# Gathering expert tokens for two pairs at once, in split precision, and reading gates and transposed one-hots from a selector product

## The chip, the cores and the metric

The kernel runs on one NeuronCore of a Trainium2 chip, as one program with one launch. The metric is the time of one execution on the device, in microseconds (us); lower is better. The reference times are the median of three executions.

## The reference, cut to what matters

One encoder layer, in float32: a mixing sub-layer (short convolution and latent attention), a cross-attention into a memory, and a mixture of 16 experts in which each expert picks its 64 tokens out of 512. The change touches only the last one.

```
h    = rmsnorm(x2, norm_moe_g)                        # x2: 512 tokens x 1024
aff  = softmax(h @ w_router)                          # 512 x 16
gates, idx = top_k(aff.T, 64)                         # per expert: 64 tokens and their gates
xg   = h[idx]                                         # 16 x 64 x 1024
a    = silu(xg @ w_gate) * (xg @ w_up)                # per expert, 1024 x 1024 each
yo   = (a @ w_down) * gates
x3   = x2 + zeros.at[idx].add(yo)                     # scatter
out  = rmsnorm(x3, norm_final_g)
```

## The kernel before, in words

The 512 tokens lie in four tiles of 128 partitions (NT = 4), the 1024 columns in eight blocks of 128 (KT = 8). Every engine runs its instructions in the order in which the code is written; nothing is rescheduled. Weights arrive by DMA in chunks of 1 MiB (128 x 2048 float32). Such a chunk lies in one of 22 slots (`NSLOT`); slots are handed out first in, first out. Every load is issued from SP's queue, in order, and an issue waits until the last reader of its slot is done. `load_experts(reserve)` (line 171 issues) hands out slots as long as more than `reserve` are free.

The experts come in eight pairs. A pair needs 24 chunks: 16 of gate and up weights, 8 of down weights. The stages of a pair are:

- `gather(p)` (lines 1241 to 1250): DVE makes a one-hot matrix `oh` (tokens x 128 picked places), multiplies it by the token's rstd into `ohr`, and TensorE multiplies x2 by it in plain float32, 4 products for each of the 8 column blocks. DVE scales each block by the norm's gain out of PSUM into `xg`.
- `gu_half` (lines 1281 and 1282): the gate and up products of half an expert, two products side by side on 64 columns of the array each; then ACT's silu (`sg`, line 1293) and DVE's product (`act`, line 1294).
- `pair_prep` (lines 1259 to 1268): the gates `gcol` and the transposed one-hot `oht` from four float32 products and four transposes of `oh`.
- `combine` (lines 1384 and 1386): the scatter of the pair before, as products with `oht`, added by DVE into `acc`.
- `down` (line 1362): four groups of 16 TensorE instructions, one for each half of the columns and of the depth. `some(each, GB)` runs two column blocks of the next pair's gather behind each group. Ahead of the first group the code runs two blocks (`some(gat, GA)`).

A plain float32 product is issued as two TensorE instructions here; a product of float32r operands as one. Elsewhere in the kernel a float32 operand is split into a float32r part and its rest (`split`, lines 119 and 120), and the products of the parts are summed. The first two experts go through `gu_wide`, with the gather of pair 0 woven between their products. Scratch tiles of 128 x 512 come from a ring of eight (`scr`), `xg` tiles from a ring of three (`mini`).

Of the kernel before, what the change touches and what calls it, by code (L numbers as in the profile page):

```python
# [18 lines left out]
KT = 8  # L19
NT = 4  # L20
# [6 lines left out]
NSLOT = 22  # L27
SPLIT_AHEAD = 2

MEM_RESERVE, RES_MM, RES_X = 4, 0, 2  # L30
MO0, MOP = 25, 4
LAG, PJ = 3, 5
GA, GB = 2, 2
WARM3, WARM, WARM2, TOP0, EV1, EV2, EV3 = 1, 4, 2, 1, 1, 2, 1


# [2 lines left out]
S_ID = S_WR + KT * E  # L39
S_SEL = S_ID + 128  # L40
S_IOTA = S_SEL + E
S_N = S_TRI = S_IOTA + C


ENTRIES = ([("cq", 0), ("cq", 1), ("ckv", 0), ("kr", 0)]
# [18 lines left out]
def layer_kernel(ctx: ExitStack, tc: tile.TileContext, x, mem, small, rope, dense, experts, out):  # L64
# [167 lines left out]
    def some(g, n):  # L232
        for _ in range(n):
            next(g, None)
# [4 lines left out]
    def col(o):  # L239
        return sm[:, o:o + 1]  # L240
# [964 lines left out]
    V.tensor_reduce(last[:, 2, 0:1], last[:, 1], axis=AX.X, op=OP.min)  # L1205


    b = Bank("warm")
    keep_warm(b, WARM)
    bt = Bank("thr")  # L1210
# [17 lines left out]
    V.tensor_tensor(pos, flag, cum, op=OP.mult)  # L1228
    V.tensor_tensor(plT, pos[:, 0], pos[:, 1], op=OP.add)
    bc.free()  # L1230
    keep_warm(b, WARM2)
    b.free()
    iota = sm[:, S_IOTA:S_IOTA + C]

    XG, gcol, OH, OHT = {}, {}, {}, {}

    def gather(p):

        w0 = OH[p] = scr(name="oh").rearrange("p (a c) -> p a c", a=NT)
        w = scr(name="ohr").rearrange("p (a c) -> p a c", a=NT)  # L1240
        V.tensor_tensor(w0.rearrange("p a (e c) -> p a e c", e=2),
                        plT[:, :, 2 * p:2 * p + 2, None].to_broadcast([128, NT, 2, C]),
                        iota[:, None, None, :].to_broadcast([128, NT, 2, C]), op=OP.is_equal)
        V.tensor_tensor(w, w0, r2[:, :, None].to_broadcast([128, NT, 128]), op=OP.mult)  # L1244
        XG[p] = mini(FT, "xg").rearrange("p (k c) -> p k c", k=KT)
        for k in range(KT):
            b = Bank("xg")
            for a in range(NT):
                PE.matmul(b.t[:, 0:128], xt[a][:, k * 128:(k + 1) * 128], w[:, a], start=a == 0, stop=a == NT - 1)  # L1249
            V.tensor_scalar(XG[p][:, k], b.t[:, 0:128], col(S_GMOE + k), None, op0=OP.mult)  # L1250
            b.free()
            yield

    def pair_prep(p):

        w = OH.pop(p)
        b = Bank("gcol")
        for a in range(NT):
            PE.matmul(b.t[:, 0:2], w[:, a], aff[:, a, 2 * p:2 * p + 2], start=a == 0, stop=a == NT - 1)
        gcol[p] = tiny(name="gcol")  # L1260
        V.tensor_copy(gcol[p][0:64], b.t[0:64, 0:1])
        V.tensor_copy(gcol[p][64:128], b.t[64:128, 1:2])
        b.free()
        b = Bank("oht")
        for a in range(NT):
            PE.transpose(b.t[:, a * 128:(a + 1) * 128], w[:, a], ident)
        OHT[p] = scr(FR, "oht")
        A.copy(OHT[p], b.t)
        b.free()


# [30 lines left out]
        gu_part(e, b, 1)  # L1302
        gu_evac(e, b, n)

    def gu_wide(e, then):

        bs = [Bank("gu") for _ in range(2)]
        for k in range(KT):
            c = xraw.popleft()
            spare = (e, k) == (0, SPARE)  # L1310
            w = c if spare else [c.t[:, j * 512:(j + 1) * 512] for j in range(4)]
            lt = XG[0][:, k, e * C:(e + 1) * C]
            for n in range(2):
                PE.matmul(bs[n].t[0:64], lt, w[n], start=k == 0, stop=k == KT - 1)  # L1314
                PE.matmul(bs[n].t[64:128], lt, w[2 + n], start=k == 0, stop=k == KT - 1)
            if not spare:
                c.free()
            load_experts(RES_X)
            then(k)
        for n in range(2):  # L1320
            gu_evac(e, bs[n], n)

    def act_trans(p, n):

        s = act.pop((p, n))
        b = Bank("actT")
        for j in range(4):
            PE.transpose(b.t[:, j * 128:(j + 1) * 128], s[:, j * 128:(j + 1) * 128], ident)
        aT[p, n] = scr(name="aT").rearrange("p (j c) -> p j c", j=4)
        w = b.t.rearrange("p (j c) -> p j c", j=4)  # L1330
        if n == 0:
            A.copy(aT[p, n], w)  # L1332
        else:
            for h in range(2):
                V.tensor_copy(aT[p, n][:, 2 * h:2 * h + 2], w[:, 2 * h:2 * h + 2])
        b.free()
# [34 lines left out]
                b.free()  # L1371
        return ys, yv

    acc_s, acc = [], []

    def combine(p, ys, yv):
        if p == 0:
            acc_s.extend(Slot(FT, "acc") for _ in range(2))
            acc.extend(acc_s[a // 2].v("a d", a=2)[:, a % 2] for a in range(NT))
        for a in range(NT):  # L1380
            for n in range(2):
                b = Bank("cb")
                for s in range(2):
                    PE.matmul(b.t, OHT[p][:, a * 128:(a + 1) * 128], yv[:, n, s], start=s == 0, stop=s == 1)  # L1384
                c = slice(n * 512, (n + 1) * 512)
                V.tensor_tensor(acc[a][:, c], b.t, (acc if p else xt)[a][:, c], op=OP.add)
                b.free()
        ys.free()

# [41 lines left out]
        if n == 1 and k == 2:  # L1431
            tail_half0(yv, [3])

    gat = gather(0)
    for _ in range(2):
        next(gat)
    pend = None
    for p in range(NP):
        last = p == NP - 1
        for q in range(2):  # L1440
            e = 2 * p + q
            if e == 0:
                gu_wide(0, lambda k: next(gat, None))
                continue
            if e == 1:
                gu_wide(1, lambda k: pair_prep(0) if k == 5 else None)
            else:
                gu_half(e, 0)
            if q == 0:
                pair_prep(p)  # L1450
                if pend is not None:
                    combine(*pend)
                    pend = None
                if last:
                    for s in xs:
                        s.free()
                    gf = Slot(FT, "gf").t
            if last and q == 1:
                preload(0)
                preload(1)  # L1460
            if e > 1:
                gu_half(e, 1, mid=(lambda: act_trans(p, 0)) if q else None)
            if last and q == 0:
                spread_gain(0)
                spread_gain(1)
        gat = iter(()) if last else gather(p + 1)
        some(gat, GA)
        if p == 0:
            act_trans(0, 0)

        def mid():
            act_trans(p, 1)
            if last:
                load_table(AF.Sqrt)

        pend = (p, *down(p, mid, gat, then=tail if last else None))
# [101 lines left out]
def _small(i):  # L1578
    s = np.zeros((128, S_N + 128), np.float32)

    def put(o, v):
        v = v.reshape(-1, 128).T
        s[:, o:o + v.shape[1]] = v

    put(S_GMIX, i["norm_mix_g"][0])
    put(S_CW, i["conv_w"][0])
    put(S_CB, i["conv_b"][0])
    put(S_QG, i["q_norm_g"][0])
    put(S_KVG, i["kv_norm_g"][0])
# [10 lines left out]
    s[:, S_IOTA:S_TRI] = np.arange(1, C + 1)  # L1600
    return s


# [27 lines left out]
```

## Time and profile before

| What | us |
|---|---|
| median of 3 executions (lowest to highest) | 1184.69 (1184.65 to 1189.49) |
| the profiled execution | 1183.84 |
| its span, first to last instruction | 1182.1 |

The profiled execution is 1.74 us longer than its span (start and end outside the program's own instructions) and 0.85 us below the median. The expert stage begins near 680 us and its last gate and up product ends near 1145 us. The views give times from the span's start. PE is TensorE, PEld its weight loads, DVE VectorE, ACT ScalarE, POOL GpSimd, SP the queue that issues the loads.

### The profile page before, as it was taken

The numbers are of one execution on the slowest core, as the hardware profiler recorded it, in microseconds if no ns is written. First come the engines' busy times: TensorE is split into PE (matmuls) and PEld (weight loads), VectorE is DVE, ScalarE is ACT, GpSimd is POOL, SyncE is SP. The second block draws the span as 40 slices with busy tenths as digits, with TensorE's granted clock in tenths as the row PEclk, the third lists the DMA queues.
The fourth block names the chain that finished last, engine by engine and source line by source line (L and its number), as shares of the span: only waits on it lengthen the run. The fifth ranks groups of instructions, "written<-read, shape, count | busy, mean of one in ns | idle before, by whom it ended". The sixth has DMA issues, their size and how long they took to land.

```text
span 1182.1 us, 13968 instructions
## 1 busy us (share of the span) xinstructions
PE 1135.1 (96%) x5715; PEld 767.9 (65%) x5715; DVE 500.0 (42%) x958; ACT 356.6 (30%) x648; POOL 1.2 (0%) x5
## 2 busy tenths in 40 slices
PE   8999999999999999999999798999999999999995
PEld 5888888888788888898888544444443444343432
DVE  6567452322687665564555712213121212121204
ACT  6223231223898734563434200101000000000013
POOL 0000000000000000000000000000000000000000
PEclk9999999999999999999999899999999999999998
DMA  8233222322010444244246788999999999999931
GB/s 345 72 107 107 72 83 96 107 107 72 1 36 2 143 143 178 72 143 142 72 179 230 311 306 325 361 399 403 421 408 421 420 422 417 421 402 421 421 144 72
DMA packets 38927, 265.95 MB, mean 225 GB/s; under 512 B 4432, under 2 KB 4816, under 8 KB 8016
## 3 DMA queue, kind: packets, MB, share of 16 engines
q1 hardware_dynamic: 38720, 265.00, 57.1%
q8 instruction: 45, 0.74, 0.3%
q14 instruction: 18, 0.15, 0.0%
q10 hardware_dynamic: 144, 0.07, 0.0%
HBM read 262.95 MB, written 2.10 MB: 224 GB/s over the span
## 4 chain that ended last, share of the span: by engine, by line
PE 92%; DVE 4%; ACT 3%; DMA 0%; issue 0%; SPq 0%; DVEq 0%
PE gu L1281 16%; PE y L1362 10%; PE xg L1249 6%; PE mm L205 4%; PE mq L205 4%; PE mo L205 4%; PE mix L205 4%; PE co L205 4%; PE gb L205 4%; PE gc L205 4%; PE gcv L205 4%; PE xc L205 4%; PE gml L205 4%; PE gu L1314 2%; PE cb L1384 2%; PE mk L205 2%
## 5 line engine op out<-in xcount | busy, mean ns | idle before, releaser
L1282 PE MATMUL gu<-xw,xg 128*64 128x512 f32 x448 | 196.8, 594 | 0.0
L1281 PE MATMUL gu<-xw,xg 128*64 128x512 f32 x448 | 196.8, 594 | 0.0
L120 DVE TENSOR_TENSOR ent<-raw,ent 128x1024 fp32r<-128x1024 f32 (+2 forms) x113 | 129.1, 1155 | 92.0 <-ACT ent L119 91.8
L1281 PEld LDWEIGHTS gu<-xw,xg 128*64 128x64 f32 x448 | 60.1, 137 | 123.4 <-issue 120.8
L1362 PE MATMUL y<-xw,aT 128*64 128x512 f32 x512 | 121.3, 608 | 0.7 <-ACT aT L1332 0.7
L119 ACT CAST ent<-raw 128x1024 fp32r<-128x1024 f32 (+2 forms) x113 | 109.0, 995 | 0.1
L1294 DVE TENSOR_TENSOR act<-gu,sg 64x512 f32<-64x512 f32 x32 | 22.2, 694 | 186.5 <-ACT sg L1293 186.4
L1249 PEld LDWEIGHTS xg<-ohr,x 128*128 128x128 f32 x512 | 63.5, 201 | 49.4 <-DVE ohr L1244 26.2
L1249 PE MATMUL xg<-ohr,x 128*128 128x128 f32 x512 | 70.6, 293 | 20.5 <-DVE ohr L1244 20.5
L1293 ACT ACTIVATE sg<-gu 64x512 f32<-64x512 f32 x32 | 18.8, 588 | 213.3 <-PE gu L1282 179.3
L1250 DVE TENSOR_SCALAR xg<-xg,small 128x128 f32<-128x128 f32 x64 | 22.5, 351 | 136.9 <-PE xg L1249 136.9
L1362 PEld LDWEIGHTS y<-xw,aT 128*64 128x64 f32 x512 | 34.9, 140 | 65.0 <-issue 61.4
L1369 ACT ACTIVATE y<-y,gcol 128x512 fp32r<-128x512 f32 x16 | 11.0, 687 | 183.7 <-PE y L1362 183.7
L1282 PEld LDWEIGHTS gu<-xw,xg 128*64 128x64 f32 x448 | 60.0, 137 | 0.0
L205 PE MATMUL mm<-ent,mo 128*128 128x512 f32 x192 | 48.4, 399 | 0.0
L205 PE MATMUL gc<-hT,ent 128*128 128x512 f32 x192 | 44.8, 389 | 0.0
L205 PE MATMUL gb<-hT,ent 128*128 128x512 f32 x192 | 44.8, 389 | 0.0
L205 PE MATMUL xc<-hT,ent 128*128 128x512 f32 x192 | 44.8, 389 | 0.0
L205 PE MATMUL gcv<-hT,ent 128*128 128x512 f32 x192 | 44.8, 389 | 0.0
L205 PE MATMUL co<-yT,ent 128*128 128x512 f32 x192 | 44.8, 389 | 0.0
L205 PE MATMUL mq<-hm,ent 128*128 128x512 f32 x192 | 44.7, 390 | 0.0
L205 PE MATMUL mo<-o,ent 128*128 128x512 f32 x192 | 44.7, 391 | 0.0
(277 smaller groups left out, 1695.7 us busy)
## 6 DMA issues: line engine op xcount, KB each, us to landing
xw<-in_experts_dram SPq DMA_DIRECT2D x189, 1024.0 KB, 9.4
raw<-in_dense_dram SPq DMA_DIRECT2D x52, 1024.0 KB, 4.8
x<-in_x_dram SPq DMA_DIRECT2D x8, 512.0 KB, 4.5
xw<-in_experts_dram SPq DMA_DIRECT2D x4, 512.0 KB, 12.1
out_dram<-out SPq DMA_DIRECT2D x4, 512.0 KB, 2.6
raw<-in_dense_dram SPq DMA_DIRECT2D x2, 512.0 KB, 8.2
mem<-in_mem_dram SPq DMA_DIRECT2D x1, 1024.0 KB, 4.8
xs<-in_experts_dram SPq DMA_DIRECT2D x4, 256.0 KB, 15.0
```

Source lines behind the costliest of these rows:

```text
L119: A.copy(hi, src)
L120: V.tensor_tensor(lo, src, f32(hi), op=OP.subtract)
L205: PE.matmul(self.o, lhsT, rhs, start=self.k == 0, stop=self.k == self.n - 1)
L1249: PE.matmul(b.t[:, 0:128], xt[a][:, k * 128:(k + 1) * 128], w[:, a], start=a == 0, stop=a == NT - 1)
L1250: V.tensor_scalar(XG[p][:, k], b.t[:, 0:128], col(S_GMOE + k), None, op0=OP.mult)
L1281: PE.matmul(b.t[0:64], lt, wg[:, k], start=kk == 0, stop=kk == KT - 1)
L1282: PE.matmul(b.t[64:128], lt, wu[:, k], start=kk == 0, stop=kk == KT - 1)
L1293: A.activation(sg[64:128], b.t[0:64], AF.Silu)
L1294: V.tensor_tensor(act[p, n][q * 64:q * 64 + 64], b.t[64:128], sg[64:128], op=OP.mult)
L1314: PE.matmul(bs[n].t[0:64], lt, w[n], start=k == 0, stop=k == KT - 1)
L1362: PE.matmul(b.t[q * 64:q * 64 + 64], aT[p, kh][:, kk, q * C:(q + 1) * C], w[:, kk], start=k == 0, stop=k == KT - 1)
L1384: PE.matmul(b.t, OHT[p][:, a * 128:(a + 1) * 128], yv[:, n, s], start=s == 0, stop=s == 1)
```

## The change

- Two gather products share one pass. `gather(ps)` takes a list of pairs: 1 and 2 behind pair 0, 3 and 4 behind pair 2, 5 and 6 behind pair 4, 7 alone behind pair 6. The one-hots of two pairs lie side by side in one float32r tile `oh` (from `mini`), so that the moving operand has 256 columns. Pair 0 keeps the old form (`gather_first`).
- The stationary operand is x2 times rstd, computed once into two slots `xn` (`norm_x2`, eight ACT instructions during expert 1), and split into a float32r part and its rest for each column block, two blocks ahead (`part`, tiles `xp`, one ACT cast and one DVE subtraction each).
- The product of a block is then eight instructions of 128 x 256. DVE scales the first pair's half into `xg`, ACT the second's.
- Ahead of the first `down` group there is no gather product any more, only the preparation.
- Gates and `oht` come from row tables: `tr` holds the affinities (float32r part and rest) and the tokens' places as 16 rows each, made once by transposes. For each pair POOL writes a selector `sel`, two products of 128 x 512 spread the pair's rows, DVE compares one with the place number (`oht`) and multiplies and sums the other (`gcol`).
- The scatter adds into x2 itself; the two `acc` slots are gone. The slots kept back by `load_experts` go from 2 to 1 (none during expert 0).

```diff
-MEM_RESERVE, RES_MM, RES_X = 4, 0, 2
+MEM_RESERVE, RES_MM, RES_X = 4, 0, 1
...
+    b_aff = to_rows(aff)
+    A.copy(tr[0:E], b_aff.t[0:E])
...
+    b_pl = to_rows(plT)
+    A.copy(tr[64:64 + E], b_pl.t[0:E])
+    b_pl.free()
     keep_warm(b, WARM2)
...
+    def to_rows(src):
+        b = Bank("rows")
+        for a in range(NT):
+            PE.transpose(b.t[0:E, a * 128:(a + 1) * 128], src[:, a], ident)
+        return b
...
+    def gather(ps):
+
+        w = len(ps) * 128
+        oh = mini(FR, "oh").rearrange("p (a c) -> p a c", a=NT)
+        for i, p in enumerate(ps):
+            one_hot(oh[:, :, i * 128:i * 128 + 128], p)
+            new_xg(p)
+        parts = {}
+
+        def part(k):
+            if k < KT:
+                parts[k] = [scr(FR, "xp").rearrange("p (a c) -> p a c", a=NT) for _ in range(2)]
+                split(xn[k // 4][:, :, k % 4 * 128:k % 4 * 128 + 128], *parts[k])
+
+        part(0)
+        part(1)
+        yield
+        for k in range(KT):
+            b = Bank("xg")
+            m = Mac(b.t[:, 0:w], 2 * NT)
+            for x in parts.pop(k):
+                for a in range(NT):
+                    m.one(x[:, a], oh[:, a, 0:w])
+            for i, p in enumerate(ps):
+                src = b.t[:, i * 128:i * 128 + 128]
+                if i == 0:
+                    V.tensor_scalar(XG[p][:, k], src, col(S_GMOE + k), None, op0=OP.mult)
+                else:
+                    A.activation(XG[p][:, k], src, AF.Copy, scale=col(S_GMOE + k))
+            b.free()
+            part(k + 2)
+            yield
...
-        w = OH.pop(p)
-        b = Bank("gcol")
-        for a in range(NT):
-            PE.matmul(b.t[:, 0:2], w[:, a], aff[:, a, 2 * p:2 * p + 2], start=a == 0, stop=a == NT - 1)
...
+        b = rows(64, 64 + E)
+        OHT[p] = scr(FR, "oht")
+        V.tensor_scalar(OHT[p], b.t, col(S_PIO), None, op0=OP.is_equal)
+        b.free()
+        b = rows(0, 32 + E)
         gcol[p] = tiny(name="gcol")
+        V.scalar_tensor_tensor(b.t, b.t, 1.0, f32(OHT[p]), op0=OP.mult, op1=OP.mult, accum_out=gcol[p])
...
-        gat = iter(()) if last else gather(p + 1)
-        some(gat, GA)
+        gat = gather(range(p + 1, min(p + 3, NP))) if p % 2 == 0 and not last else iter(())
         if p == 0:
             act_trans(0, 0)
+        next(gat, None)
```

What moves on the engines is shown at three places. The first is TensorE at the end of pair 4 (experts 8 and 9), before the change: `gu` is the last gate and up product, `xg` the gather for pair 5, `y` the first `down` group.

```order
L1282 MATMUL gu_6707<-xw_6581,xg_6462 64x512
L1249 MATMUL xg_6747<-ohr_6743,x_3169 128x128 x2
L1249 MATMUL xg_6747<-ohr_6743,x_3170 128x128 x2
L1249 MATMUL xg_6753<-ohr_6743,x_3169 128x128 x2
L1249 MATMUL xg_6753<-ohr_6743,x_3170 128x128 x2
L1362 MATMUL y_1110_6760<-xw_6583,aT_6725 64x512
```

And TensorE at the same place in the changed program (between the second row and the last four stand the other seven `y` products of the first group).

```order
L1348 MATMUL gu_6745<-xw_6611,xg_6207 64x512
L1428 MATMUL y_1131_6794<-xw_6624,aT_6763 64x512
...
L206 MATMUL xg_6805<-oh_6780,xp_6785 128x256 x4
L206 MATMUL xg_6805<-oh_6780,xp_6786 128x256 x4
L206 MATMUL xg_6820<-oh_6780,xp_6789 128x256 x4
L206 MATMUL xg_6820<-oh_6780,xp_6790 128x256 x4
```

The products that need DVE's one-hot no longer stand between the last `gu` and the first `y`; a whole `down` group stands ahead of them.

The second place is DVE beside it, before the change.

```order
L1294 TENSOR_TENSOR act_6675<-gu_6707,sg_6739 64x512
L1241 TENSOR_TENSOR oh_6742<-plT_5419,small_75 128x512
L1244 TENSOR_TENSOR ohr_6743<-oh_6742,r_721_4967 128x512
L1250 TENSOR_SCALAR xg_6746<-xg_6747,small_75 128x128
L1250 TENSOR_SCALAR xg_6746<-xg_6753,small_75 128x128
```

DVE in the changed program, same place.

```order
L1360 TENSOR_TENSOR act_6713<-gu_6745,sg_6777 64x512
L1255 TENSOR_TENSOR oh_6780<-plT_5427,small_75 128x4x128 x2
L121 TENSOR_TENSOR xp_6786<-xn_5555,xp_6785 128x512
L121 TENSOR_TENSOR xp_6790<-xn_5555,xp_6789 128x512
L1310 TENSOR_SCALAR xg_6782<-xg_6805,small_75 128x128
L121 TENSOR_TENSOR xp_6817<-xn_5555,xp_6816 128x512
L1310 TENSOR_SCALAR xg_6782<-xg_6820,small_75 128x128
L121 TENSOR_TENSOR xp_6832<-xn_5555,xp_6831 128x512
```

Two one-hots and two subtractions now follow `act` ahead of the first scaling, and one subtraction follows each scaling.

The third place is TensorE in `pair_prep` of pair 5, before: the gates, the transposes, and the scatter of pair 4.

```order
L1259 MATMUL gcol_6885<-aff_4968,oh_6742 128x2 x4
L1266 MATMUL oht_6893<-small_75,oh_6742 128x128 x4
L1384 MATMUL cb_6900<-y_6759,oht_6614 128x512 x2
```

And after the change.

```order
L1325 MATMUL rows_6997<-tr_5403,sel_6995 128x512
L1325 MATMUL rows_7001<-tr_5403,sel_6995 128x512
L1447 MATMUL cb_7005<-y_6793,oht_6648 128x512 x2
```

Two products that read POOL's selector stand where four float32 products and four transposes stood.

## Rows read from the trace of the kernel before

**Rows 1.** The page's head and its part 1, the whole execution.

```profile
span 1182.1 us, 13968 instructions
...
PE 1135.1 (96%) x5715; PEld 767.9 (65%) x5715; DVE 500.0 (42%) x958; ACT 356.6 (30%) x648; POOL 1.2 (0%) x5
```

**Rows 2.** The chain that ended last, shares by engine.

```profile
PE 92%; DVE 4%; ACT 3%; DMA 0%; issue 0%; SPq 0%; DVEq 0%
```

**Rows 3.** Stages: length, busy time of five engines, PEclk, DMA share, GB/s.

```profile
682.00:720.00 38.00, 37.37 (x195) 16.09 (x193) 5.04 (x13) 2.93 (x5) 0.00 (x0) 1.00 0.87 328
720.00:760.00 40.00, 37.08 (x206) 19.72 (x208) 12.94 (x26) 3.14 (x6) 0.00 (x0) 1.00 0.84 325
760.00:843.00 83.00, 77.53 (x386) 33.59 (x382) 17.58 (x33) 7.25 (x12) 0.00 (x0) 0.98 0.99 401
843.00:904.00 61.00, 57.87 (x293) 26.64 (x293) 14.54 (x29) 4.90 (x8) 0.00 (x0) 0.97 1.01 415
904.00:963.00 59.00, 56.27 (x292) 25.66 (x292) 14.24 (x28) 4.90 (x8) 0.00 (x0) 1.00 1.01 421
963.00:1024.00 61.00, 57.99 (x293) 26.98 (x294) 14.41 (x29) 4.90 (x8) 0.00 (x0) 0.97 1.01 419
1024.00:1085.00 61.00, 58.13 (x295) 26.73 (x296) 14.33 (x28) 4.90 (x8) 0.00 (x0) 0.97 1.01 411
1085.00:1134.00 49.00, 49.00 (x268) 24.19 (x268) 11.55 (x24) 4.31 (x7) 0.00 (x0) 1.00 1.00 412
1134.00:1138.00 4.00, 4.00 (x16) 1.28 (x14) 0.69 (x1) 0.59 (x1) 0.00 (x0) 1.00 0.04 14
```

**Rows 4.** The chain in order of time, end of pair 3: start, length, what.

```profile
901.17 0.60 ACT sg L1293
...
903.99 2.05 PE xg L1249 x16
906.04 3.58 PE y L1362 x16
...
926.76 0.42 PE gu L1281
...
933.63 0.98 PE gcol L1259 x8
934.62 0.49 PE oht L1266 x4
935.11 3.67 PE cb L1384 x16
```

**Rows 5.** TensorE's waits on others, 720 to 1182 us: total, times, longest.

```profile
PE xg L1249 <- DVE ohr L1244: 20.1, 7, 2.9
```

**Rows 6.** The chain in order of time, end of pair 1.

```profile
782.55 3.56 PE xg L1249 x16
786.11 3.66 PE y L1362 x16
```

**Rows 7.** Groups by form, whole execution: busy us, mean ns, idle before.

```profile
L1249 PE MATMUL xg<-ohr,x 128*128 128x128 f32 x512 | 70.6, 293 | 20.5 <-DVE ohr L1244 20.5
...
L1384 PE MATMUL cb<-y,oht 128*128 128x512 f32 x112 | 27.3, 396 | 0.0
...
L205 PE MATMUL mk<-mT,ent 128*128 128x256 f32 x192 | 24.1, 284 | 0.0
...
L1250 DVE TENSOR_SCALAR xg<-xg,small 128x128 f32<-128x128 f32 x64 | 22.5, 351 | 136.9 <-PE xg L1249 136.9
...
L120 DVE TENSOR_TENSOR yT<-scr,yT 128x512 fp32r<-128x512 f32 x8 | 5.5, 693 | 5.5 <-ACT yT L119 5.5
...
L119 ACT CAST yT<-scr 128x512 fp32r<-128x512 f32 x8 | 5.0, 622 | 69.7 <-DVE scr L467 69.7
```

**Rows 8.** The expert weights' loads, from issue to landing.

```profile
DMA to landing us min/median/max: 4.7/9.4/18.5
```

**Rows 9.** The chain in order of time, from the last pair's first `down` product.

```profile
1145.10 0.85 PE y L1362 x2
```

More of the change, by code (lines that the diff above doesn't have):

```diff
@@ L28 @@
 SPLIT_AHEAD = 2
-MEM_RESERVE, RES_MM, RES_X = 4, 0, 2
+MEM_RESERVE, RES_MM, RES_X = 4, 0, 1
 MO0, MOP = 25, 4
 LAG, PJ = 3, 5
-GA, GB = 2, 2
+GB = 2
 WARM3, WARM, WARM2, TOP0, EV1, EV2, EV3 = 1, 4, 2, 1, 1, 2, 1
@@ L41 @@
 S_IOTA = S_SEL + E
-S_N = S_TRI = S_IOTA + C
+S_PIO = S_IOTA + C
+S_N = S_TRI = S_PIO + 1
 ENTRIES = ([("cq", 0), ("cq", 1), ("ckv", 0), ("kr", 0)]
@@ L1205, in layer_kernel @@
     V.tensor_reduce(last[:, 2, 0:1], last[:, 1], axis=AX.X, op=OP.min)
+    tr = scr(FR, "tr")
+    nc.gpsimd.memset(f32(tr)[0:32], 0.0)
+    def to_rows(src):
[5 more added lines that the diff above has]
+    A.copy(tr[0:E], b_aff.t[0:E])
     b = Bank("warm")
@@ L1233, in layer_kernel, with one_hot, new_xg, gather_first @@
     iota = sm[:, S_IOTA:S_IOTA + C]
[L1235 to L1241, printed above, removed]
+    XG, gcol, OHT = {}, {}, {}
+    xn_s, xn = [], []
+    def one_hot(o, p):
+        V.tensor_tensor(o.rearrange("p a (e c) -> p a e c", e=2),
                         plT[:, :, 2 * p:2 * p + 2, None].to_broadcast([128, NT, 2, C]),
                         iota[:, None, None, :].to_broadcast([128, NT, 2, C]), op=OP.is_equal)
+    def new_xg(p):
+        XG[p] = mini(FT, "xg").rearrange("p (k c) -> p k c", k=KT)
+    def gather_first():
+        w0 = scr(name="oh").rearrange("p (a c) -> p a c", a=NT)
+        w = scr(name="ohr").rearrange("p (a c) -> p a c", a=NT)
+        one_hot(w0, 0)
         V.tensor_tensor(w, w0, r2[:, :, None].to_broadcast([128, NT, 128]), op=OP.mult)
-        XG[p] = mini(FT, "xg").rearrange("p (k c) -> p k c", k=KT)
+        V.tensor_tensor(tr[32:32 + E], b_aff.t[0:E], f32(tr)[0:E], op=OP.subtract)
+        b_aff.free()
+        new_xg(0)
         for k in range(KT):
@@ L1249, in gather, with norm_x2 @@
                 PE.matmul(b.t[:, 0:128], xt[a][:, k * 128:(k + 1) * 128], w[:, a], start=a == 0, stop=a == NT - 1)
-            V.tensor_scalar(XG[p][:, k], b.t[:, 0:128], col(S_GMOE + k), None, op0=OP.mult)
+            V.tensor_scalar(XG[0][:, k], b.t[:, 0:128], col(S_GMOE + k), None, op0=OP.mult)
             b.free()
             yield
-    def pair_prep(p):
-        w = OH.pop(p)
-        b = Bank("gcol")
-        for a in range(NT):
-            PE.matmul(b.t[:, 0:2], w[:, a], aff[:, a, 2 * p:2 * p + 2], start=a == 0, stop=a == NT - 1)
-        gcol[p] = tiny(name="gcol")
[L1261 to L1268, printed above, removed]
+    def norm_x2(i):
+        h, a = divmod(i, NT)
+        A.activation(xn[h][:, a], xt[a][:, h * 512:h * 512 + 512], AF.Copy, scale=r2[:, a:a + 1])
@@ new lines, in pair_prep, with rows @@
+    def pair_prep(p):
+        sel = scr(FR, "sel")[:, 0:128]
+        nc.gpsimd.tensor_copy(sel.rearrange("p (e c) -> p e c", e=2),
+                              sm[:, S_SEL + 2 * p:S_SEL + 2 * p + 2, None].to_broadcast([128, 2, C]))
+        def rows(lo, hi):
+            b = Bank("rows")
+            PE.matmul(b.t, sel[lo:hi], tr[lo:hi], start=True, stop=True)
+            return b
+        b = rows(64, 64 + E)
[3 more added lines that the diff above has]
+        b = rows(0, 32 + E)
+        gcol[p] = tiny(name="gcol")
+        V.scalar_tensor_tensor(b.t, b.t, 1.0, f32(OHT[p]), op0=OP.mult, op1=OP.mult, accum_out=gcol[p])
@@ L1303, in gu_half, with gu_wide @@
         gu_evac(e, b, n)
-    def gu_wide(e, then):
+    def gu_wide(e, then, reserve):
         bs = [Bank("gu") for _ in range(2)]
@@ L1317, in gu_wide @@
                 c.free()
-            load_experts(RES_X)
             then(k)
+            load_experts(reserve)
         for n in range(2):
@@ L1372, in down @@
         return ys, yv
-    acc_s, acc = [], []
+    acc = xt
     def combine(p, ys, yv):
-        if p == 0:
-            acc_s.extend(Slot(FT, "acc") for _ in range(2))
-            acc.extend(acc_s[a // 2].v("a d", a=2)[:, a % 2] for a in range(NT))
         for a in range(NT):
@@ L1385, in combine @@
                 c = slice(n * 512, (n + 1) * 512)
-                V.tensor_tensor(acc[a][:, c], b.t, (acc if p else xt)[a][:, c], op=OP.add)
+                V.tensor_tensor(acc[a][:, c], b.t, acc[a][:, c], op=OP.add)
                 b.free()
@@ L1432, in tail, with spread_x2 @@
             tail_half0(yv, [3])
-    gat = gather(0)
+    gat = gather_first()
     for _ in range(2):
         next(gat)
+    def spread_x2(k):
+        if k < 2:
+            xn_s.append(Slot(FT, "xn"))
+            xn.append(xn_s[k].v("a c", a=NT))
+        elif k < 6:
+            norm_x2(2 * k - 4)
+            norm_x2(2 * k - 3)
     pend = None
@@ L1442, in layer_kernel @@
             if e == 0:
-                gu_wide(0, lambda k: next(gat, None))
+                gu_wide(0, lambda k: next(gat, None), 0)
                 continue
             if e == 1:
-                gu_wide(1, lambda k: pair_prep(0) if k == 5 else None)
+                gu_wide(1, spread_x2, RES_X)
             else:
                 gu_half(e, 0)
-            if q == 0:
+            if q == 0 or e == 1:
                 pair_prep(p)
@@ L1454, in layer_kernel @@
                 if last:
-                    for s in xs:
+                    for s in xn_s:
                         s.free()
@@ L1599, in _small @@
         s[32 * g:32 * g + E, S_SEL:S_SEL + E] = np.eye(E)
-    s[:, S_IOTA:S_TRI] = np.arange(1, C + 1)
+    s[:, S_IOTA:S_PIO] = np.arange(1, C + 1)
+    s[:, S_PIO] = np.arange(128) % C + 1
     return s
```

## The prediction

> **What bounds the kernel now.** I read the page's head and its busy times first: TensorE is busy for 96% of the span and no other engine for half of it [rows 1]. The chain that ended last agrees, 92% of it lies on PE [rows 2]. Both say that time taken from TensorE is time taken from the kernel, as long as nothing stands close behind. So I cut the expert stage into its pairs and looked at the DMA column [rows 3]. The reader should see two things there. From 760 us on the loads run at 401 to 421 GB/s with a DMA share of 0.99 to 1.01, and they stop near 1134 us, when the last pair's gate and up products are still running. A pair takes 24 chunks of 1 MiB, 25.17 MB. At 421 GB/s, the most that a stage shows, that is 59.8 us; the pairs of the trace take 59 to 61 us. TensorE is the bound, but the loads are a second bound less than 2% below it, and TensorE never waits for them only because it works on chunks that landed long before.
>
> Then I read where a pair's TensorE time goes. In the chain, between the last gate and up product of pair 3 and the next product, stand ACT's silu at 901.17, DVE's product and DVE's two one-hot steps; the gather begins at 903.99 [rows 4]. The waits of TensorE put a number on all of these: 20.1 us in seven waits of up to 2.9 us, all on `ohr` [rows 5]. After four of the last six waits TensorE is also slow for a while: behind pair 1 the first gather and the first `down` group take 3.56 and 3.66 us [rows 6] against 2.05 and 3.58 us behind pair 3 [rows 4]. The granted clock shows the same, 0.97 to 0.98 in those four stages and 1.00 in the one from 904 us [rows 3].
>
> **The change part by part, first for TensorE alone.**
> - The wait on `ohr`: a whole `down` group of 3.58 us [rows 4] now stands ahead of the first gather. DVE meanwhile does `act`, two one-hots and two subtractions, and 0.69 us is what such an operation takes [rows 7]; from the last product these are 0.6 (silu) and five times 0.7, 4.1 us, and the first block needs only the first four, 3.4 us. All 20.1 us go. If that cover were gone, up to 0.6 us a gather would come back, four times.
> - The slow clock behind the waits: 7.22 less 5.63 is 1.6 us, four times, 6.4 us. It goes with the waits.
> - The gather: before, 64 instructions a pair, 16 in 2.05 us [rows 4], so 8.2 us. Now 64 instructions serve two pairs. The nearest row of such a product (float32r, 256 columns) is `mk`, 24.1 us for 192, 125 ns each [rows 7], 8.0 us for two pairs. Three double passes save 3 x 8.4 = 25 us.
> - The single pass for pair 7 has float32r with 128 columns, which no row shows. Below, half of `mk`'s price, 4.0 us; above, as much as 512 columns (`cb`, 27.3 us for 112, 244 ns [rows 7]), 15.6 us. The old gather, also 128 columns, is the nearest row, so I take no difference.
> - Gates and transposed one-hots: 0.98 and 0.49 us [rows 4] become two products of 512 columns, 0.49 us by `cb`. Eight times 0.98 is 7.8 us. The selector on POOL has no row; POOL is busy for 1.2 us in all [rows 1] and the tile that it overwrites is read for the last time well before, so I take nothing. If TensorE waited for it, it would be about 1 us a pair.
> - The row tables ahead of expert 0: the four transposes of the places stand before the two warming products, 0.5 us by `oht` [rows 4]. I count 0.5 us against the change.
> - Splitting x2 for the gather: 32 casts on ACT of 0.62 us and 32 subtractions on DVE of 0.69 us [rows 7]. DVE is busy for 14 of 61 us in a pair and ACT for 5 [rows 3], so 8 blocks of both fit beside two gathers' `down` groups, two blocks ahead of their use. Nothing on the path. The eight scalings of x2 run beside expert 1.
>
> Sum for TensorE: 20.1 + 6.4 + 25 + 7.8 less 0.5 is 59 us. If TensorE alone decided, the profiled 1183.84 us would become 1125 us.
>
> **The same change against the loads.** An average pair would then take TensorE about 52 us, and the loads still need 59.8. So TensorE eats its lead and meets the loads. What is left to load is read from the stages: from 760 us on, length times GB/s gives 33.28 + 25.32 + 24.84 + 25.56 + 25.07 + 20.19 + 0.06, 154.3 MB [rows 3]. At 421 GB/s without a break this takes 366.5 us, so the data end at 1126.5 us instead of 1134. I take 760 us as the start of unbroken loading because TensorE's pace before it does not change: during expert 0 the old gather stays, and behind pair 0 a double pass takes the time of the old single one. The two slots for `xn` are taken from the weights in the same stretch, and the smaller reserve gives one back. The bound on the other side is that the loads also fill what is open between 682 and 760 us, 0.13 of 38 us and 0.16 of 40 us [rows 3], 11 us earlier.
>
> The end follows from the last pair. Its `down` chunks are the last 8 MiB, 19.9 us of loading, so the last gate and up chunk has its data at 1106.6 us. From issue to landing a load takes at least 4.7 us [rows 8], of which the transfer at 421 GB/s is 2.5, so I add 2.2: 1108.8 us. Its two chunks are worth 8 pieces of 0.43 us [rows 4], 3.4 us, which ends at 1112.2. The first `down` group waits for two more chunks, 5.0 us behind, until 1113.8 us. Before, it began at 1145.10 [rows 9]. What follows it is unchanged, and its chunks come every 5.0 us, faster than TensorE uses them there. The end moves by 31.3 us, 1183.84 to 1152.5. The median shown stands 0.85 us above the profiled execution, less than this sum is good for; I say **1152 us**, 2.7% faster. Of TensorE's 59 us some 27 come back as waits for weights, in pairs 4 to 7.
>
> The loading rate is the figure that decides. The row says 421 GB/s for one core [rows 3]. The Trainium skill (DMA: Bandwidth & Descriptors, Specifications) gives a fabric ceiling of 435 GB/s, and a limit of about 358 GB/s for a core's share of the memory. The trace stands above the second, so that one does not hold here. By the first, the 154.3 MB would take an estimated 355 us and the end would be near 1141 us.
>
> **The rivals.**
> - *TensorE's whole saving shows, 1125 us.* It needs the loads to be no bound: 154.3 MB in about 339 us, 455 GB/s. No stage shows more than 421 [rows 3]. Chance 0.04.
> - *The loads run earlier or faster, 1141 us.* The 11 us above. For it: the reserve is smaller and TensorE frees slots sooner. Against it: TensorE's pace in that stretch stays. Chance 0.12.
> - *The clock falls in the waits for weights, 1160 to 1175 us.* A wait of 2.9 us was followed by the lower level, 1.2 instead of 2.4 GHz, in four cases of six, at 1.6 us each [rows 4, 6]. The new waits are some 40, one for each two chunks, of 1.5 us at most (5.0 less 3.4). A fall costs nothing while TensorE would wait anyway; if a fall followed half of the 40 waits and half of it could not be absorbed, 16 us remain. Against it: the new waits are half as long as those that showed falls. Chance 0.13. The Trainium skill (TensorE: Matmul & The Clock Gate, HAM oscillation) tells of a loop that waits for loads between its products and starts each round at the lower clock; no row here shows it for waits this short.
> - *Slower: TensorE stays at 1.2 GHz through the loading-bound stretch.* Its place is 905 to 1112 us, 180 us of TensorE work at full clock beside 27 us of waits. Work at the lower level takes twice its time. It decides from the point where this costs 27 + 31 us, so when 58 of the 180 us run slow, a mean clock of about 0.76; if all ran slow, the time would be near 1300 us. Against it: the lowest clock of a stage is 0.97 [rows 3], and a slow TensorE no longer waits. Chance 0.04.
> - *No gain: the split chain stalls each block, about 1183 us.* If a block waited for ACT's cast, DVE's subtraction and the scaling before it (0.62 + 0.69 + 0.35 us [rows 7]), 32 blocks cost 53 us, which takes TensorE alone back to 1178. It needs the two blocks of lead to be useless. Chance 0.05.
>
> **How the numbers follow.** The forecast, loads as the second bound, has 0.62: 1152 us, its own range 1146 to 1159. With the two faster rivals (0.16) and the clock (0.13) the cases below 1177 hold 0.91. A range of 1140 to 1165 takes in the forecast, the earlier loads and the milder half of the clock's cases, some 0.8. A change of 0.5%, 6 us, is about what a measurement here can tell from none. Faster 0.91, same 0.05 (the split chain), slower 0.04.
>
> **What would show it.** The wait on `ohr` is gone, and TensorE's waits name the weight loads instead, some 20 to 30 us in all, none above 2 us, from pair 4 on. The DMA column stands at 421 until about 1126 us. The double gather shows 192 products of 256 columns at 125 ns. The clock is 1.00 from 760 us to the last pair. I am wrong if the stages show over 430 GB/s, if TensorE waits for `sel`, `xp` or `xg`, or if the clock is below 0.95 in the last four pairs.

## The result, and the profile after

| | before | changed |
|---|---|---|
| median (lowest to highest), us | 1186.09 (1184.65 to 1189.49) | 1152.74 (1151.92 to 1154.87) |
| profiled execution / its span, us | 1183.84 / 1182.1 | 1154.87 / 1153.1 |

The ratio is 0.972, with a 95% interval of 0.969 to 0.975: the change made the kernel 33 us faster. The profiled execution of the changed kernel is the slowest of the four by 2 us, so its times run a little late.

First the head of the page, the TensorE line, the GB/s of its 40 slices and the chain (to be read against [rows 1, 2]).

```profile
span 1153.1 us, 13577 instructions
...
PE 1115.3 (97%) x5451; PEld 742.3 (64%) x5451; DVE 515.4 (45%) x968; ACT 383.7 (33%) x706; POOL 4.0 (0%) x14
...
GB/s 353 74 110 87 96 73 110 77 93 122 1 37 1 74 183 201 55 111 182 74 117 142 287 305 322 357 409 421 421 421 421 421 420 420 423 421 421 420 420 122
...
PE 76%; DMA 18%; DVE 3%; ACT 3%; issue 0%; SPq 0%; DVEq 0%; ACTq 0%
```

The busy share hardly tells the two kernels apart, 97% against 96%. The chain does: 92% of it lay on PE before, 76% now, and 18% lies on DMA. The stages show where (the windows view; the last two columns are DMA share and GB/s, the one before them is the granted clock), against [rows 3].

```profile
682.00:720.00 38.00, 38.00 (x195) 16.61 (x193) 4.46 (x11) 6.80 (x12) 0.29 (x1) 0.99 0.73 272
720.00:760.00 40.00, 39.33 (x202) 19.73 (x204) 20.53 (x39) 9.92 (x21) 0.29 (x1) 1.00 0.93 368
760.00:843.00 83.00, 83.00 (x404) 33.12 (x401) 21.02 (x38) 11.43 (x22) 0.29 (x1) 1.00 1.01 420
843.00:904.00 61.00, 61.00 (x286) 23.49 (x284) 15.03 (x26) 7.86 (x15) 0.59 (x2) 1.00 1.01 421
904.00:963.00 59.00, 56.20 (x272) 25.30 (x272) 20.29 (x37) 11.24 (x23) 0.29 (x1) 1.00 1.01 421
963.00:1024.00 61.00, 54.32 (x230) 20.61 (x227) 11.27 (x19) 4.32 (x7) 0.29 (x1) 0.97 1.01 421
1024.00:1085.00 61.00, 58.33 (x284) 25.50 (x282) 19.12 (x36) 9.07 (x15) 0.29 (x1) 1.00 1.01 421
1085.00:1128.00 43.00, 43.00 (x185) 16.66 (x182) 9.77 (x17) 5.60 (x9) 0.00 (x0) 1.00 0.99 411
```

From 766 us on a chunk lands about every 2.49 us, with no gap above 3.4 us until the last one, at 1131 us. TensorE waits from 904 to 1085 us, and the view of its waits (total, times, longest, in us) names the weights; `ohr` [rows 5] is gone from it.

```profile
PE y L1428 <- DMA xw<-in_experts_dram: 6.4, 5, 1.3
PE gu L1348 <- DMA xw<-in_experts_dram: 5.7, 5, 2.2
PE fin L1470 <- ACT y L1435: 1.6, 2, 0.8
PE y L1428 <- ACT aT L1398: 0.7, 1, 0.7
```

The end of pair 2 (timeline of PE; start and length) shows the new order at work, where [rows 4] had a silu, an `act` and two one-hot steps on the chain: the first `down` group follows the last gate and up product, the double gather follows the group, and nothing waits.

```profile
825.46 0.59 PE L1348 MATMUL gu<-xw,xg 128*64 128x512 f32 x1
825.88 3.60 PE L1428 MATMUL y<-xw,aT 128*64 128x512 f32 x16
829.41 2.18 PE L206 MATMUL xg<-oh,xp 128*128 128x256 f32 x16
```

The new groups by shape, with count, busy time and the mean of one record (records overlap, so the price of one is busy time by count), beside [rows 7]:

```profile
L206 PE MATMUL xg<-oh,xp 128*128 128x256 f32 x192 | 26.1, 289 | 0.0
...
L1274 PE MATMUL xg<-ohr,x 128*128 128x128 f32 x64 | 8.9, 285 | 0.0
L206 PE MATMUL xg<-oh,xp 128*128 128x128 f32 x64 | 8.0, 278 | 0.0
...
L1325 PE MATMUL rows<-tr,sel 48*128 48x512 f32 x8 | 4.0, 499 | 0.0
L1325 PE MATMUL rows<-tr,sel 16*128 16x512 f32 x8 | 4.0, 496 | 0.0
```

The gathers take 43.0 us of TensorE in place of 70.6, of which some 4 us before were the slow clock behind the waits. The selector products have records of 0.50 us each and follow each other at 0.43.

Ahead of the expert stage the changed kernel loses time. The timeline of PE there:

```profile
679.08 0.65 PE L1216 MATMUL rows<-small,plT 128*16 128x128 f32 x4 [0.73 <-DVE plT L1242]
679.51 3.57 PE L279 MATMUL warm<-one 128*128 128x512 f32 x4
682.92 1.95 PE L1274 MATMUL xg<-ohr,x 128*128 128x128 f32 x16
```

The transposes wait 0.73 us for `plT`, and behind them the warming products take 3.57 us; in the kernel before they follow `cum` at once and take 1.94 us. 3.57 us is close to twice that, and the windows view shows the lower of the clock's two levels (third figure from the end, 0.51):

```profile
679.50:683.00 3.50, 3.50 (x7) 1.45 (x6) 1.53 (x3) 0.57 (x1) 0.00 (x0) 0.51 0.69 258
```

The first gather begins 2.25 us later than before. Not every execution shows the slow products: of the seven profiled ones with this prologue, all with the same wait of 0.73 us, two do (this one and the one with two slots kept back). In the other five the warming products take 1.9 us, and the first gather begins at 681.1 to 681.9 us, 0.4 to 1.3 us later than before.

### The profile page after: what moved, and what is told of

Same layout as the page of the kernel before. It is cut to its first block, busy times and chain, and to the rows that moved or that the text cites. A ratio compares the mean times of both kernels' runs of the same rounds, so it can differ in the third digit from the quotient of the medians.

```text
span 1153.1 us, 13577 instructions
## 1 busy us (share of the span) xinstructions
PE 1115.3 (97%) x5451; PEld 742.3 (64%) x5451; DVE 515.4 (45%) x968; ACT 383.7 (33%) x706; POOL 4.0 (0%) x14
## 4 chain that ended last, share of the span: by engine, by line
PE 76%; DMA 18%; DVE 3%; ACT 3%; issue 0%; SPq 0%; DVEq 0%; ACTq 0%
DMA xw<-in_experts_dram 17%; PE gu L1347 8%; PE y L1428 6%; PE mm L206 4%; PE mo L206 4%; PE mq L206 4%; PE mix L206 4%; PE co L206 4%; PE gcv L206 4%; PE gb L206 4%; PE gc L206 4%; PE xc L206 4%; PE gml L206 4%; PE gu L1380 2%; PE xg L206 2%; PE mk L206 2%
## 5 line engine op out<-in xcount | busy, mean ns | idle before, releaser
L1348 PE MATMUL gu<-xw,xg 128*64 128x512 f32 x448 | 200.2, 599 | 5.8 <-DMA xw<-in_experts_dram 5.7
L1347 PE MATMUL gu<-xw,xg 128*64 128x512 f32 x448 | 200.0, 599 | 0.0
L1347 PEld LDWEIGHTS gu<-xw,xg 128*64 128x64 f32 x448 | 59.4, 137 | 99.5 <-issue 96.0
L1348 PEld LDWEIGHTS gu<-xw,xg 128*64 128x64 f32 x448 | 59.4, 137 | 32.1 <-issue 17.8
L206 PE MATMUL mix<-ent,mx 128*128 128x512 f32 x192 | 44.0, 390 | 0.0
L206 PE MATMUL gml<-hT,ent 128*128 128x512 f32 x192 | 43.8, 389 | 0.0
L206 PEld LDWEIGHTS co<-yT,ent 128*128 128x128 f32 x192 | 36.0, 188 | 7.5
L206 PEld LDWEIGHTS gc<-hT,ent 128*128 128x128 f32 x192 | 36.0, 188 | 7.5
```

Of the source, the lines that this page charges most:

```text
L206: PE.matmul(self.o, lhsT, rhs, start=self.k == 0, stop=self.k == self.n - 1)
L1347: PE.matmul(b.t[0:64], lt, wg[:, k], start=kk == 0, stop=kk == KT - 1)
L1348: PE.matmul(b.t[64:128], lt, wu[:, k], start=kk == 0, stop=kk == KT - 1)
```

## The experiments

T1 is the prediction's theory: the loads are the second bound, and TensorE's time counts only where the loads wait for slots that TensorE frees. T2 says that the loads bind little and the gain is the plain sum of TensorE's savings. The kernel before measured 1184.8 to 1185.6 us beside these runs.

| kernel | median us | ratio to before (95%) |
|---|---|---|
| changed, half of the gate and up loads | 1130.06 | 0.954 (0.951 to 0.956) |
| before, half of the gate and up loads | 1185.64 | 1.001 (0.999 to 1.002) |
| before, new order alone | 1157.31 | 0.977 (0.975 to 0.979) |
| changed, stall put back | 1160.38 | 0.979 (0.977 to 0.981) |
| changed, 8 extra products early | 1159.44 | 0.978 (0.977 to 0.980) |
| changed, 8 extra products late | 1152.05 | 0.972 (0.971 to 0.973) |
| changed, two slots kept back | 1152.87 | 0.972 (0.971 to 0.974) |
| changed, transposes later | 1151.48 | 0.971 (0.970 to 0.973) |
| changed, one slot less | 1154.79 | 0.974 (0.972 to 0.976) |
| changed, transposes later, gain spread early | 1150.62 | 0.970 (0.968 to 0.972) |
| the same without two warming products | 1147.51 | 0.968 (0.966 to 0.970) |

### Fewer loads, in the changed kernel and in the one before

```diff
-        cg, cu = xraw.popleft(), xraw.popleft()
+        cg = xraw.popleft()
+        cu = cg if e > 1 else xraw.popleft()
...
-        cu.free()
...
+            if i >= PAIR_CHUNKS and i % PAIR_CHUNKS < 16 and i % 2:
+                st["xchunk"] += 1
+                continue
```

> The changed kernel, but from pair 1 on the up products read the gate chunk and the up chunks are not loaded (the computation is changed in that; TensorE runs the same instructions). This takes 56 MiB of 154.3 MB out of the loads behind pair 0. T1 (the loads are the second bound and end the gain): TensorE alone is left, the predicted sum of 59 us less about 4.6 us that the trace after shows as mis-sized (selector products 0.61 instead of 0.98 us saved a pair, prologue 2.25 instead of 0.5 us late), so about 1186 - 54 = 1132 us, between 1126 and 1135, and no wait of TensorE on a weight load. T2 (the loads bind nothing beyond the 12 us of waits that TensorE itself shows, TensorE's savings were simply smaller): 1140 us or more. T0 (loads play no part): 1153 us.

> The same cut of the loads in the kernel before (the up products read the gate chunk from pair 1 on; same TensorE instructions). T1: TensorE was its bound and never waited for a load, so no change, 1183 to 1187 us, with the waits on ohr still 20 us. If the loads had bound the kernel before as well, it would be faster by more than 6 us, and the gain of the change would not be what the sum says.

The changed kernel came to 1130.06 us, inside T1's 1126 to 1135 and 10 us below T2's. The kernel before did not move: 1185.64 us. So the loads cost the changed kernel 22.7 us and the old one nothing. That the old one stood still also shows that fewer loads don't make TensorE's products faster by themselves. Of the changed kernel with fewer loads, the TensorE line and the two stages in which weights were waited for:

```profile
PE 1104.0 (98%) x5451; PEld 738.7 (65%) x5451; DVE 515.3 (46%) x968; ACT 383.3 (34%) x706; POOL 4.0 (0%) x14
```

```profile
904.00:963.00 59.00, 59.00 (x296) 27.52 (x295) 22.84 (x43) 11.22 (x23) 0.29 (x1) 1.00 0.88 341
963.00:1024.00 61.00, 61.00 (x283) 22.20 (x283) 15.62 (x27) 4.91 (x8) 0.29 (x1) 1.00 0.86 331
```

TensorE is busy throughout at clock 1.00. T2 had its ground in the waits view, which names only 12.1 us. The two spans differ by 24.1 us, of which idle time is 12.8 (37.8 against 25.0) and busy time 11.3 (1115.3 against 1104.0), for the same 5451 instructions. From the first gather on they differ by 23.0 us: 12.1 are the waits that the view names, 1.7 the slow stretch shown further down, and some 9 stand in the records as busy time. The starts of the products, laid side by side for the two executions, show where. As a rule a gate product (L1347) and an up product (L1348), on their two halves of the array, start together every 0.43 us. Where the up chunk lands later than the gate chunk (here at 900.77 us), gate products go ahead alone, and at the end as many up products are left to run alone (timeline of PE of the changed kernel):

```profile
900.06 1.02 PE L1347 MATMUL gu<-xw,xg 128*64 128x512 f32 x2
900.82 0.64 PE L1348 MATMUL gu<-xw,xg 128*64 128x512 f32 x1
...
903.44 1.02 PE L1348 MATMUL gu<-xw,xg 128*64 128x512 f32 x2
```

Each time this costs steps of 0.4 to 0.5 us in which TensorE is busy with half of the array. So the waits view is a lower bound here.

### The new order alone, and the old stall in the new kernel

In the kernel before, `gather` gets a `yield` ahead of its first product (pair 0 takes one step more for it):

```diff
-GA, GB = 2, 2
+GA, GB = 1, 2
...
         XG[p] = mini(FT, "xg").rearrange("p (k c) -> p k c", k=KT)
+        yield
         for k in range(KT):
...
-    for _ in range(2):
+    for _ in range(3):
...
-        some(gat, GA)
         if p == 0:
             act_trans(0, 0)
+        some(gat, GA)
```

In the changed kernel two blocks run ahead of the first `down` group again:

```diff
-        next(gat, None)
+        some(gat, 3)
```

> The kernel before with one part of the change alone: the first down group stands ahead of the gather, whose one-hots are made meanwhile. T1: the 20.1 us of waits on ohr and the 6.4 us of slow clock behind them go, 1186 - 26.5 = 1159.6 us, between 1157 and 1162, near the loads' bound but above it. T2 (savings just add): the same here, but then all other parts together bring only 7 us. If the waits move to another place (a block waiting for its scaling or for xw), above 1165 us.

> The changed kernel with the stall put back: two blocks of the gather stand ahead of the first down group behind pairs 0, 2, 4 and 6, so TensorE waits each time for silu, act, one-hot and split, 3.4 to 4.1 us, with 1.6 us of slow clock behind some. T1: the wait behind pair 0 counts, since the loads there still wait for slots; those behind pairs 2, 4 and 6 lie where the loads end the time: 1153 + 4 to 5, so 1155 to 1159 us. T2 (everything adds): 4 x 4 to 5.5 us, so 1169 to 1175 us.

The order alone brings 27.5 us (1184.79 to 1157.31), near the 26.5 us of the prediction's first two terms. All other parts together, worth 27.2 us of TensorE by the run with fewer loads (1184.79 less 1130.06 less 27.5), then bring only 4.6 us more. That is what a second bound does. The windows of the new order alone show that it already stands at that bound, with TensorE busy and the loads unbroken at once:

```profile
904.00:963.00 59.00, 59.00 (x314) 27.79 (x312) 14.77 (x30) 5.58 (x9) 0.00 (x0) 1.00 1.01 421
963.00:1024.00 61.00, 61.00 (x321) 28.11 (x318) 15.38 (x31) 5.59 (x9) 0.00 (x0) 1.00 1.01 420
```

The stall put back costs 7.6 us, above T1's 2 to 6 and far below T2's 16 to 22. Its waits and the stage of the first one:

```profile
PE xg L206 <- DVE oh L1255: 10.8, 4, 2.9
PE gu L1348 <- DMA xw<-in_experts_dram: 4.2, 4, 1.3
PE y L1428 <- DMA xw<-in_experts_dram: 3.7, 3, 1.3
```

```profile
720.00:730.00 10.00, 7.63 (x30) 4.82 (x32) 5.31 (x11) 2.90 (x7) 0.00 (x0) 0.66 0.35 149
```

The stall behind pair 0 (2.88 us) was followed by the lower clock, 0.66 over these 10 us. The two groups behind it show the price (timeline of PE of this run):

```profile
722.37 3.75 PE L206 MATMUL xg<-oh,xp 128*128 128x256 f32 x16 [2.88 <-DVE oh L1255]
726.05 4.67 PE L1428 MATMUL y<-xw,aT 128*64 128x512 f32 x16
```

At full clock they take 2.18 and 3.65 us, so 2.6 us are lost and not the 1.6 us I had counted. The last weight lands 452.9 us after the first gather's start, against 446.8 to 448.1 us in three runs without a stall: 5 to 6 us, near the 2.9 and 2.6 of this one stall. The other 2 us fit the stall behind pair 6, at 1060.29 us (2.2 us): it lies behind the last wait for weights, where nothing absorbs it. The two stalls between, 2.86 and 2.83 us, left no trace in the time.

### Extra work early and late

```diff
             some(each, GB)
+            if (p, i) == (0, 1):
+                bx = Bank("warm")
+                keep_warm(bx, 8)
+                bx.free()
```

The late one has `(4, 1)`.

> The changed kernel with eight extra products of 128 x 512 (the warming ones, 0.97 us each, 7.8 us) behind the second down group of pair 0, near 735 us, where the loads still wait for slots that TensorE frees. T1: this delay moves the whole stream of loads, 1153 + 6 to 8 us, so 1159 to 1161 us. T2 (everything adds): 1161 us. If only the total of the loads mattered and not when they start: 1153 us.

> The same eight extra products behind the second down group of pair 4, near 1000 us, between TensorE's waits for weights. T1: TensorE has that time to spare (the visible waits behind 1000 us are 7.4 us, and the unseen ones as much again), the loads go on, no more than 1.5 us is added: 1152.5 to 1154.5 us. T2 (everything adds): 1161 us.

The extra products in the early run's timeline of PE:

```profile
732.76 7.06 PE L279 MATMUL warm<-one 128*128 128x512 f32 x16
```

And in the late run's:

```profile
944.72 7.06 PE L279 MATMUL warm<-one 128*128 128x512 f32 x16
```

The late work lies at 945 us, not near 1000 as the expectation put it; that is still between the waits for weights (920 to 1056 us). The 7.06 us near 735 us cost 6.7 us (1159.44 against 1152.74), the same work at 945 us cost nothing (1152.05). This tells T1 from T2 without touching a load: what a TensorE microsecond is worth depends on where it lies.

### What a slot is worth

Two slots kept back (`RES_X` 1 to 2), and one slot really taken away:

```diff
+            if k == 2:
+                hold.append(Slot(FT, "hold"))
```

> The changed kernel with two slots kept back instead of one, as before the change. T1: one chunk fewer is loaded while the loads wait for slots, so the stream ends 2.5 us later: 1155 to 1156 us. If the slots don't matter: 1153 us.

> The changed kernel with one slot taken out of use from expert 1 on (handed out, never written, given back in the last pair). Keeping two slots back instead of one changed nothing (the loads were issued at the same times to 0.1 us from the 24th to the 60th), so what is kept back is no slot less; this one is. T1: while the loads wait for slots each load waits for the slot that comes free one chunk later, 2.5 us, and the stream ends 2.5 us later: 1152.5 + 2.5, between 1154 and 1156.5 us. If the number of slots doesn't matter: 1152.5 us.

Keeping back two changed nothing (1152.87 us), so T1's first reading of a slot fell. The loads' issue times say why: counted from the first gather, the load numbered 24 (the first 1 MiB load is 0) is issued at 15.7 us, 40 at 66.0 and 60 at 106.7 in both kernels. Of those between, a single one differs by more than 0.1 us: 37.0 in place of 35.3. Slots are handed out first in, first out, while the code is written; on the chip SP runs ahead and each load waits only for its own slot's last reader. The number kept back decides who gets which slot, not how many are in use. With a slot really taken away each load goes where the next one went (number 39 at 66.0 us in place of 60.7); this cost 2.05 us by the median, near one chunk's 2.49.

### Two moves that make it faster

The transposes behind the warming products; then also `gf` and `spread_gain` in pair 5 instead of the last pair; then also `WARM3` 0.

```diff
-    b_pl = to_rows(plT)
-    A.copy(tr[64:64 + E], b_pl.t[0:E])
-    b_pl.free()
     keep_warm(b, WARM2)
     b.free()
+    b_pl = to_rows(plT)
+    A.copy(tr[64:64 + E], b_pl.t[0:E])
+    b_pl.free()
...
+                if p == NP - 3:
                     gf = Slot(FT, "gf").t
...
-            if last and q == 0:
+            if p == NP - 3 and q == 0:
                 spread_gain(0)
...
-WARM3, WARM, WARM2, TOP0, EV1, EV2, EV3 = 1, 4, 2, 1, 1, 2, 1
+WARM3, WARM, WARM2, TOP0, EV1, EV2, EV3 = 0, 4, 2, 1, 1, 2, 1
```

> The changed kernel with the four transposes of the places behind the two warming products instead of ahead of them, so that TensorE doesn't wait for plT and the warming products don't run at the lower clock. The first gather then starts near 680.8 us, 2.1 us earlier. T1: time of TensorE in this stretch counts fully, 1150.5 us, between 1150 and 1151.2. If the loads alone set the end wherever TensorE is: 1153 us.

> The changed kernel with the transposes of the places behind the warming products, and with the 2.05 us of products that spread the last norm's gain moved from the last pair to pair 5, where TensorE waits for weights. Behind the last wait for weights, near 1056 us, TensorE works without a break to the end, so this time counts until the last down chunks bind (the first down group's second chunk lands 0.2 us before TensorE comes to it, and its use is 1.5 us further on). T1: 1151.5 - 1.5 = 1150 us, between 1149 and 1151. If the landing of the last chunks alone sets the end: 1151.5 us.

> The same, and without the two warming products (1.06 us each by their rows) in the first two down groups of the last pair. T1: 1 to 2 us less than the kernel with the two moves, 1148 to 1149.5 us. If the waits that appear in their place bring the lower clock, the same or slower, 1150 to 1153 us.

The first move brings 1.3 us by the medians (1151.48), less than the 2.1 us expected, which stood on an execution with slow warming products. Its timeline shows the warming products at full speed and the transposes in the gap behind them:

```profile
677.61 1.94 PE L279 MATMUL warm<-one 128*128 128x512 f32 x4
679.39 0.60 PE L1216 MATMUL rows<-small,plT 128*16 128x128 f32 x4
679.95 2.02 PE L1274 MATMUL xg<-ohr,x 128*128 128x128 f32 x16
```

The first gather starts at 679.95 us; in the six other profiled runs with the changed kernel's prologue it starts between 681.1 and 683.0 us, so the profiled execution (682.92) was among the late ones. The second move brings 0.9 us more (1150.62) of the 2.05 us moved. In its profiled execution the second chunk of the first `down` group lands at 1113.30 us, 0.94 us later than in the run with the first move alone (1112.36), which fits the missing part; its products begin at 1113.58, right behind the first warming product, so the weights nearly bind there. Around the second warming product this run shows:

```profile
1118.60 1.07 PE L1428 MATMUL y<-xw,aT 128*64 128x512 f32 x2
1119.61 1.13 PE L279 MATMUL warm<-one 128*128 128x512 f32 x2
1120.66 3.65 PE L1428 MATMUL y<-xw,aT 128*64 128x512 f32 x14
```

Without the warming products the time falls by another 3.1 us, more than their 2.1, to 1147.51 us. In that run's timeline of PE, a wait for the chunk stands where the first of them stood, and the clock stays at 1.00 up to 1128 us:

```profile
1111.19 1.02 PE L1428 MATMUL y<-xw,aT 128*64 128x512 f32 x2
1112.95 3.65 PE L1428 MATMUL y<-xw,aT 128*64 128x512 f32 x14 [0.74 <-DMA xw<-in_experts_dram]
...
1117.98 3.65 PE L1428 MATMUL y<-xw,aT 128*64 128x512 f32 x16
```

This is the fastest version run, 5 us below the changed kernel. The rows show why the gain exceeds the products' own time. A warming product stands between the first products of the two experts, which otherwise run side by side on the two halves of the array. With it the group takes 5.71 us (from 1118.60), without it 3.65, so the second one cost 2.06 us and not 1.06. Of the first, the wait for the chunk leaves 0.25 us. The other 0.4 us between the two profiled executions (2.66 us by their spans) lie ahead of it: the first `down` group began at 1111.19 and not at 1111.57 us.

## Why the prediction was right, step by step

The forecast was 1152 us for a measured 1152.74, and by the mechanism that it named: TensorE's savings meet the loads. That it came within 1 us is in part luck, as the last step below shows.

- **The wait on `ohr` and the slow clock behind it**, 26.5 us: the order alone gave 27.5. All of the wait is gone.
- **The gather**, 25 us: 23.4 at full clock. The old gathers take 70.6 us with the slow clock, which the first term has counted already, and 66.4 us in the kernel with the new order alone; the new ones take 43.0. A product of 256 columns costs 136 ns (26.1 us by 192) where the row of `mk` said 125; the single pass costs 125 ns for 128 columns, so the choice of "no difference" to the old pass (8.0 against 8.2 us) held.
- **Gates and one-hots**, 7.8 us: mis-sized. I took 0.49 us for both selector products; they follow each other at 0.43 us each, so a pair saves 0.61 us, 4.9 us in all. `cb` was the wrong nearest row. Why such a product takes 0.43 us is open: a bank's start alone doesn't explain it, since `cb` starts a new bank every second product and still steps at 0.23 us.
- **The row tables**, 0.5 us against: mis-sized, 0.4 to 1.3 us in five profiled executions with this prologue, 2.25 us and more in two, and 1.3 us by the medians when undone. I had counted the transposes and not the wait ahead of them, nor that the warming products would run slow in some executions.
- **Splitting x2 and the selector on POOL**, nothing: held. In the expert stage TensorE's products wait for none of `sel`, `xp` and `xg`.
- **The sum for TensorE**, 59 us: 54.7 by the run with fewer loads (1184.79 less 1130.06). The terms as measured give the same: 27.5 + 23.4 + 4.9 less 1.2, the later start of that run's first gather, is 54.6.
- **The loads**, 154.3 MB at 421 GB/s: the rate stood as read. Loads before 760 us moved little, 25.06 MB against 25.46 between 682 and 760, as assumed: the loads of expert 1 are issued 3 to 9 us later than before, counted from the first gather, and from number 44 on at least 3 us earlier. But the smaller reserve did not give a slot back, as I had written: two slots kept back instead of one changed nothing (the reserve of none during expert 0 was not tested by itself).
- **The waits for weights**, some 27 us, none above 2: 23 by the run with fewer loads, of which the waits view shows 12.1; the longest was 2.2. The clock was to be 1.00 from 760 us on; it was, but for 0.97 from 963 to 1024 us.
- **The end** is where the working was less right than its number. I had the last pair wait for its weights down to the first `down` group. The last wait in the trace ends at 1056.42 us, in pair 6. From there to the last pair's first `down` group TensorE works without a break, a few us behind the landings, and reaches that group just when its second chunk is there, without waiting for it: the chunk landed at 1116.02, the group began at 1116.26 (predicted 1113.8, in an execution that started 2.25 us late), and the first product that reads this chunk came at 1118.27 us, behind the warming product. The landing came as predicted; that TensorE's own 59.8 us from 1056.42 on ended at the same time was luck. Pair 7 has no gather behind it but has the old pair's scatter, the gain's spreading and the preloads. So there are three stretches: up to 766 us TensorE's time counts through the slots, from there to 1056 us the loads alone count, and then TensorE's time counts again.

Of the rivals, the clock's fall in the waits for weights showed once. After the longest wait the products ran slow, with steps of 0.85 us instead of 0.43, 1.7 us lost (timeline of PE of the changed kernel):

```profile
1016.65 0.64 PE L1348 MATMUL gu<-xw,xg 128*64 128x512 f32 x1 [2.16 <-DMA xw<-in_experts_dram]
...
1017.68 1.06 PE L1348 MATMUL gu<-xw,xg 128*64 128x512 f32 x1
...
1019.39 1.06 PE L1348 MATMUL gu<-xw,xg 128*64 128x512 f32 x1
```

It lies where TensorE has time to spare, and the next wait, at 1046.48 us, took it up. The nine shorter waits, up to 1.33 us, were followed by products at the full rate. The loop that the Trainium skill tells of (TensorE: Matmul & The Clock Gate, HAM oscillation) starts every round at the lower clock. It waits some 3 to 5 us each round; no wait for weights here was as long.

## What to carry to other kernels

When the busiest engine has a second bound 2% behind it, add up the savings, then work out the second bound's time from bytes and the rate of its best stage, and forecast the later of the two. A microsecond saved or spent is worth what its stretch makes it worth: mark the stretches by which wait ends last, and put extra work where another bound already makes the engine wait. To learn what a bound costs, take its load away and leave the instructions: the waits view showed half of it. And look at which products run side by side: what separated a pair of them here cost more than its own time.

## What the runs showed that I had not expected

- Of the 23.0 us that the loads cost, some 9 stand in the records as busy time: products that run side by side fall out of step when one's chunk lands later.
- A warming product put between two that run side by side cost 2.06 us, twice its own 1.06.
- A float32r product with 128 columns took as long as the reference row with 256 (125 ns), and 256 columns took 136 ns in the gather.
- In the prologue the products behind a wait of 0.73 us ran at the lower clock (3.57 instead of 1.94 us) in two profiled executions of seven and at the higher one in five, with the same wait and the same instructions. So the wait alone does not decide it; what does, no run shows.
- The number of slots kept back in the program changed one issue time, by 1.7 us, and not the result; one slot fewer cost 2 us.
